# An unused 64-byte tile among the constants: the address that weights and moving operands have modulo 512 bytes

## The chip, the cores and the metric

The kernel runs on one core of one Trainium2 chip. The metric is the device time of one execution, in microseconds (us). Beside the timed runs there is one profiled execution, from which all traces and profile pages here come.

## The reference

One layer of a hybrid mixer on 1024 latent tokens and 256 context tokens of width 1024, all in float32:

```python
h, gate = modulate(x, c, norm_g, w_ada, b_ada)          # RMSNorm, adaLN scale and shift
z  = h @ w_in                                           # 1024 x 1024 -> 1024 x 8704
ya = neighbourhood_attention(q, k, v, kc, vc, rpb) * silu(z_a)   # 16 x 64 grid, 8 x 16 window, + 256 context keys
yb = b * dw_conv(c_ * v_, w_short) * silu(z_b)          # short depthwise convolution, width 3
yc = silu(layer_norm(dw_conv(a * sigmoid(g), w_conf))) * silu(z_c)   # depthwise convolution, width 31
m  = ga * (ya @ w_out_a) + gb * (yb @ w_out_b) + gc * (yc @ w_out_c) # sigmoid gates, 1024 wide
x  = x + gate * (m @ w_o)
```

## The kernel before

The kernel keeps float32 accuracy by cutting every matrix operand into two float32r parts, `hi` and `lo` (a rounded copy made by ScalarE, and the rest by a subtraction on VectorE or GpSimd). Each product is three matmuls: `hi*hi`, `hi*lo`, `lo*hi`. Each matmul has its own weight load. Most have 128 x 128 weights and a moving operand of 128 x 512:

```python
106    def mm3(ps, terms):
109            pe.matmul(ps, ah, bh, start=i == 0, stop=False)
110            pe.matmul(ps, ah, bl, start=False, stop=False)
111            pe.matmul(ps, al, bh, start=False, stop=i == n - 1)
...
841    def product(ps, w, blocks, first, last):
846            pe.matmul(ps, wh, bh, start=first and j == 0, ...)
847            pe.matmul(ps, wh, bl, start=False, ...)
848            pe.matmul(ps, wl, bh, start=False, ...)
```

The second operand of `pe.matmul` is the weights, the third the moving operand. In the profile's rows the moving operand stands first: `gc<-T,wh` has moving `T` and weights `wh`.

The work, in the order of time in the profiled execution:

- **0 to 115 us**: norms, adaLN and the first query, key and value projection (L417 to L419), whose weights are the tokens `ha`/`hb` and whose moving operand is the weight matrix `wh`/`wl`, 384 wide. Beside it the first GLU (`glu_steps`, L291), with weights `grow`, `ghi`, `glo` and moving `ha`/`hb`, 512 wide.
- **115 to 521 us**: attention for four pairs of heads, and woven into it by the scheduler the projections of the next pair (L109 to L111 with `ps`, 384 wide), the GLUs 1 to 3 (L109 to L111 with `gps`, `aps`, 512 wide) and, from 340 us, the first quarters of the later products (`quarter_part`, L677 to L679, 512 wide).
- **521 to 890 us**: `group` (L864) after `group`, each a 2 x 2 block product in a seven-product scheme, all matmuls 512 wide (`product`, L846 to L848). VectorE adds the sums out of PSUM (L852, L895, L899), GpSimd and VectorE make weight sums and `lo` parts (L760, L763), and between them VectorE does the width-31 convolution, 124 steps of 128 x 1024 (`conv_steps`, L820 and L822), which ends at 820 us. The very first two products of this part take weights that were made ahead of time (`ah`, `al`, L794); all later ones take `wh` and `wl` from `wsplit` (L835).
- **890 to 1030 us**: three merges of the branches (`merge`, L1152), 12 matmuls for each of 16 half rows, and beside them the LayerNorm's column sums (L1213, L1214, weights `onesr`).
- **1030 to 1117 us**: the last product with `w_o` (`fin_first`, `fin_rest`), again `product`, and the output.

**Where the tiles lie.** SBUF tiles come from pools that are stacked from two ends. On the left lies first the pool of constants `cst`, whose size is the sum of its tiles; behind it `hT` (`ha0` to `ha7`, `hb0` to `hb7`: the moving operands of most products), and behind that the pools of each stage (`a1`, `st`, `at`; later `tp`, `sp`, `bp`). On the right lie `edge`, `rp`, and the pools that hold the weights: `w` up to 521 us and `wq` after it.

```python
53    cst = ctx.enter_context(tc.tile_pool(name="cst", bufs=1))
54    hp_pool = ctx.enter_context(tc.tile_pool(name="hT", bufs=1, reuse_waits="tile"))
55    edge = ctx.enter_context(tc.tile_pool(name="edge", bufs=1, side="right"))
56    edge.tile([P, 32], F32, name="edge")
57    rp = ctx.enter_context(tc.tile_pool(name="rp", bufs=6, side="right"))
59    wp = wctx.enter_context(tc.tile_pool(name="w", bufs=9, side="right"))
801    wq = ctx.enter_context(tc.tile_pool(name="wq", bufs=1, side="right", reuse_waits="tile"))
```

Addresses in the built program, in bytes within a partition. Nearly all tiles behind `cst` are multiples of 512 bytes long, and one column block of weights (128 float32r) is 512 bytes, so that whole groups of tiles share one address modulo 512:

| tiles | first address before | modulo 512 | in the changed kernel | modulo 512 |
|---|---|---|---|---|
| `ha0` (and all of `hT`) | 3360 | 288 | 3424 | 352 |
| `grow` (pool `a1`) | 81184 | 288 | 81248 | 352 |
| `T1` (pool `tp`) | 68896 | 288 | 68960 | 352 |
| `ah`, `al` (pool `sp`) | 136480 | 288 | 136544 | 352 |
| `qd`, `ks`, `vs`, `phi`, `pt` (pool `at`) | 147232 (`qd`) | 288 | 147296 | 352 |
| `wh`, `wl` (pool `w`) | 184672 | 352 | 184672 | 352 |
| `wh`, `wl` (pool `wq`) | 171872, 188256 | 352 | 171872, 188256 | 352 |
| `ident` (pool `cst`) | 1376 | 352 | 1376 | 352 |

So before, weights from `w` and `wq` lie 64 bytes above their moving operands modulo 512 (the **64 class**: L677 to L679, nearly all of L846 to L848, L109 to L111 with `gps`, `aps` and `ops`). In the projections the weights are the tokens and lie 64 bytes below their moving `wh`, `wl` (the **-64 class**). Where both operands come from the left pools they lie at one address (the **0 class**: attention's L586 to L596 and L634, the first GLU, the two products with `ah` and `al`, the column sums).

Of the kernel before, what the change touches and what calls it, by code (L numbers as in the profile page):

```python
# [8 lines left out]
F32 = mybir.dt.float32  # L9
# [8 lines left out]
P = 128  # L18
D = 1024
KT = 8  # L20
# [27 lines left out]
def tile_hybrid(ctx: ExitStack, tc, x, xT, cx, cond, crow, ng, w_ada, b_ada, wqkv, wz,  # L48
# [4 lines left out]
    cst = ctx.enter_context(tc.tile_pool(name="cst", bufs=1))  # L53
# [18 lines left out]
    def const(src, shape, name):  # L72
        t = cst.tile(shape, F32, name=name)
        nc.sync.dma_start(t, src)
        return t
# [232 lines left out]
    with tc.tile_pool(name="st", bufs=1) as st, tc.tile_pool(name="ps_t", bufs=1, space=PSUM) as pst:  # L308
# [14 lines left out]
            return t.rearrange("p (a n) -> p a n", a=2)  # L323

        cond_t = const(cond, [P, KT, 2], "cond_t")
        act.activation(cond_t, cond_t, AF.Silu)

        def silu_rows(i):
# [1160 lines left out]
def build(ins):  # L1489
    import concourse.bacc as bacc  # L1490

    nc = bacc.Bacc("TRN2", target_bir_lowering=False, num_devices=1, dynamic_dma_scratch_size=1024)
    aps = {n: nc.dram_tensor(f"in_{n}", v.shape, F32, kind="ExternalInput").ap() for n, v in ins.items()}
    out = nc.dram_tensor("out_0", (KT, P, S), F32, kind="ExternalOutput").ap()
    with tile.TileContext(nc, schedule_with_timeline_sim=True) as tc:
        tile_hybrid(tc, **aps, out=out)
    return nc
# [11 lines left out]
```

## Time and profile before

| | |
|---|---|
| median of 3 runs | 1121.47 us (1115.14 to 1122.44) |
| profiled execution, its own time | 1118.38 us |
| span of its trace | 1116.6 us |
| TensorE (PE) busy | 1083.6 us, 97% of the span, 5270 matmuls |
| weight loads (PEld) | 908.2 us |
| VectorE (DVE), GpSimd (POOL), ScalarE (ACT) busy | 787.4, 656.8, 551.3 us |
| mean granted TensorE clock | 0.992 |

A matmul's duration in the trace runs to its modelled end and overlaps the next matmul. How fast PE works through a queue of matmuls is therefore read from the starts: the **pitch**, the time from one matmul's start to the next one's.

### The profile page before, as it was taken

Reading aid. Unit: us, or ns where it says so; the run is one execution under the profiler, and the core shown is the slowest. Engines: PE = TensorE matmul, PEld = TensorE weight load, DVE = VectorE, ACT = ScalarE, POOL = GpSimd, SP = SyncE. Lnnn points to the kernel's source line nnn. Section 1 sums busy time; section 2 is a strip of 40 time slices with the busy share of each in tenths; the row PEclk is TensorE's granted clock in tenths of the full one; section 3 lists DMA queues with packets and bytes.
Section 4 is the critical chain, followed back from the end, with each engine's and each line's share of the span. In section 5 each row is a group of like instructions: output and inputs, shape, how many; then the busy total and the mean of one; then the engine's idle time right before and its main releaser. Section 6 shows DMA issues by size and latency. Waiting matters only on the chain.

```text
span 1116.6 us, 15993 instructions
## 1 busy us (share of the span) xinstructions
PE 1083.6 (97%) x5270; PEld 908.2 (81%) x5270; DVE 787.4 (71%) x1255; ACT 551.3 (49%) x1172; POOL 656.8 (59%) x666
## 2 busy tenths in 40 slices
PE   6899999999999999999999989999999999999998
PEld 5688898998998778887888768778888888788886
DVE  6985476667666754426995998997953459878664
ACT  6865566576567576655432233133344434425630
POOL 3245956447536963334998857887777461623660
PEclk8999999999999999999999989999999999999999
DMA  9629423213303454449456436466445988461362
GB/s 352 214 74 293 129 68 126 92 49 99 120 28 98 163 198 133 135 159 367 144 165 181 153 104 200 154 203 189 160 161 165 322 323 302 132 238 65 97 219 100
DMA packets 92995, 186.26 MB, mean 167 GB/s; under 512 B 11792, under 2 KB 36752, under 8 KB 92816
## 3 DMA queue, kind: packets, MB, share of 16 engines
q1 hardware_dynamic: 88304, 183.13, 48.9%
q10 hardware_dynamic: 4608, 2.10, 0.6%
q8 instruction: 42, 0.69, 0.3%
q14 instruction: 41, 0.34, 0.1%
HBM read 136.96 MB, written 50.79 MB: 168 GB/s over the span
## 4 chain that ended last, share of the span: by engine, by line
PE 75%; DVE 8%; DMA 6%; POOL 5%; issue 3%; ACT 2%; SPq 1%; POOLq 0%; DVEq 0%; ACTq 0%
PE ops L110 4%; PE ops L109 4%; PE ops L111 4%; PE gd L846 3%; PE gd L848 3%; PE gd L847 3%; PE qps L678 3%; PE qps L679 3%; PE qps L677 3%; PE py L634 3%; DVE cv L822 3%; PE pp L614 3%; PE ps L109 2%; PE ps L110 2%; PE ps L111 2%
## 5 line engine op out<-in xcount | busy, mean ns | idle before, releaser
L822 DVE SCALAR_TENSOR_TENSOR cv<-upad,cf_t,cv 128x1024 f32<-128x1024 f32 x120 | 153.5, 1279 | 1.0
L759 ACT CAST wh<-s 128x512 fp32r<-128x512 f32 x111 | 66.6, 616 | 133.2 <-POOL s L763 80.8
L92 POOL TENSOR_TENSOR wl<-wr,wh 128x384 fp32r<-128x384 f32 (+1 forms) x87 | 85.8, 992 | 73.2 <-ACT wh L90 58.9
L760 POOL TENSOR_TENSOR wl<-s,wh 128x512 fp32r<-128x512 f32 x83 | 113.6, 1379 | 11.8 <-ACT wh L759 11.8
L617 DVE TENSOR_TENSOR plo<-pp,phi 128x256 fp32r<-128x256 f32 (+2 forms) x96 | 54.4, 575 | 41.7 <-ACT phi L616 40.8
L90 ACT CAST wh<-wr 128x384 fp32r<-128x384 f32 (+1 forms) x96 | 45.8, 483 | 40.7 <-PE qps L678 23.4
L679 PE MATMUL qps<-ha,wl 128*128 128x512 f32 x160 | 64.0, 400 | 0.0
L678 PE MATMUL qps<-ha,wh 128*128 128x512 f32 x160 | 63.8, 399 | 0.0
L677 PE MATMUL qps<-ha,wh 128*128 128x512 f32 x160 | 63.7, 399 | 0.0
L573 POOL TENSOR_TENSOR bias<-mk,img 64x96 f32<-64x96 bf16 (+1 forms) x96 | 45.2, 477 | 26.6 <-DVE mn L599 18.1
L616 ACT CAST phi<-pp 128x256 fp32r<-128x256 f32 (+2 forms) x96 | 46.4, 494 | 21.6 <-PE pp L614 21.2
L760 POOL TENSOR_TENSOR wl<-wro,wh 128x512 fp32r<-128x512 f32 x12 | 17.1, 1425 | 55.8 <-ACT wh L759 48.7
L599 DVE CUSTOM_DVE_ANT_0 pt<-sl,bias,mn 128x384 f32<-128x384 f32 (+1 forms) x64 | 37.2, 581 | 17.1 <-PE sl L596 14.8
L614 PE MATMUL pp<-ident,pt 128*128 128x128 f32 x304 | 47.2, 272 | 1.0 <-DVE pt L607 1.0
L846 PE MATMUL gd<-hb,wh 128*128 128x512 f32 x96 | 39.3, 409 | 7.1 <-DVE c L852 7.1
L614 PEld LDWEIGHTS pp<-ident,pt 128*128 128x128 f32 x304 | 37.8, 141 | 9.5 <-issue 1.4
L600 ACT ACTIVATE pt<-sc,mn 128x256 f32<-128x256 f32 x64 | 30.5, 477 | 29.8 <-DVE mn L599 27.8
L80 POOL TENSOR_SCALAR ssh<-ssh 128x4 f32<-128x4 f32 (+1 forms) x40 | 10.2, 255 | 59.3 <-DVE ssh L255 56.5
L81 POOL TENSOR_TENSOR ssh<-ssh,half_neg 128x4 f32<-128x4 f32 (+1 forms) x40 | 39.9, 998 | 3.0
L760 DVE TENSOR_TENSOR wl<-s,wh 128x512 fp32r<-128x512 f32 x28 | 36.0, 1287 | 7.6 <-ACT wh L759 7.5
L607 DVE TENSOR_SCALAR pt<-pt,mn 128x640 f32<-128x640 f32 (+1 forms) x64 | 40.5, 675 | 1.0
L109 PE MATMUL ps<-wh,hb 128*128 128x384 f32 x112 | 38.9, 348 | 0.5 <-ACT raw L175 0.4
(439 smaller groups left out, 3793.7 us busy)
## 6 DMA issues: line engine op xcount, KB each, us to landing
wr<-in_wz SPq DMA_DIRECT2D x34, 512.0 KB, 3.9
gs<-gd SPq DMA_DIRECT2D x24, 512.0 KB, 5.2
wr<-in_wz SPq DMA_DIRECT2D x52, 192.0 KB, 2.5
wada<-in_w_ada SPq DMA_DIRECT2D x16, 512.0 KB, 8.6
wrf<-in_wo SPq DMA_DIRECT2D x16, 512.0 KB, 3.5
cht<-chd SPq DMA_DIRECT2D x24, 256.0 KB, 3.1
wro<-in_wout SPq DMA_DIRECT2D x24, 256.0 KB, 4.3
p1d<-quarter SPq DMA_DIRECT2D x20, 256.0 KB, 2.5
```

Source lines behind the costliest of these rows:

```text
L92: lo_eng.tensor_tensor(out=lo[:, :n], in0=raw[:, :n], in1=hi[:, :n].bitcast(F32), op=ALU.subtract)
L109: pe.matmul(ps, ah, bh, start=i == 0, stop=False)
L110: pe.matmul(ps, ah, bl, start=False, stop=False)
L111: pe.matmul(ps, al, bh, start=False, stop=i == n - 1)
L614: pe.transpose(out=pp[:, c * P : c * P + P], in_=src, identity=ident)
L677: pe.matmul(ps, wh, bh, start=k == 0, stop=False, skip_group_check=True)
L678: pe.matmul(ps, wh, bl, start=False, stop=False, skip_group_check=True)
L679: pe.matmul(ps, wl, bh, start=False, stop=k % 4 == 3, skip_group_check=True)
L759: act.copy(hi, src)
L760: eng.tensor_tensor(out=lo, in0=src, in1=hi.bitcast(F32), op=ALU.subtract)
L822: dve.scalar_tensor_tensor(out=acc, in0=src, scalar=cf_t[:, i, j : j + 1], in1=acc, op0=ALU.mult, op1=ALU.add)
L846: pe.matmul(ps, wh, bh, start=first and j == 0, stop=False, skip_group_check=True)
```

## The change

A tile of 128 x 8 x 2 float32, 64 bytes in each partition, is taken from `cst` behind `cond_t`. Nothing writes or reads it. The constants allocated behind it, and every pool of the left side, move up by 64 bytes; the right side and the constants ahead of it stay. All instructions, their order on every engine and their waits are the same in both programs; only addresses differ. In the changed kernel the 64 class and the -64 class both become the 0 class.

```diff
         cond_t = const(cond, [P, KT, 2], "cond_t")
+        cst.tile([P, KT, 2], F32, name="sig")
         act.activation(cond_t, cond_t, AF.Silu)
```

## The prediction

> **What bounds the kernel now.** I read the page first: the span, the busy time and the chain that ended last.
>
> ```profile
> span 1116.6 us, 15993 instructions
> PE 1083.6 (97%) x5270; PEld 908.2 (81%) x5270; DVE 787.4 (71%) x1255; ACT 551.3 (49%) x1172; POOL 656.8 (59%) x666
> PE 75%; DVE 8%; DMA 6%; POOL 5%; issue 3%; ACT 2%; SPq 1%; POOLq 0%; DVEq 0%; ACTq 0%
> ```
>
> TensorE carries three quarters of the chain, so what a matmul costs in a full queue decides. Its duration doesn't say that; the pitch does. The timeline of PE around 521 us, where the 64 class and the 0 class follow each other, is the most telling view of this trace (columns: start us, duration us):
>
> ```profile
> 519.53 0.39 PE L679 MATMUL qps<-ha,wl 128*128 128x512 f32 x1
> ...
> 521.63 0.40 PE L679 MATMUL qps<-ha,wl 128*128 128x512 f32 x1
> 521.86 0.39 PE L846 MATMUL ga<-ha,ah 128*128 128x512 f32 x1
> ...
> 522.55 0.39 PE L846 MATMUL ga<-ha,ah 128*128 128x512 f32 x1
> ...
> 527.31 0.40 PE L846 MATMUL gc<-T,wh 128*128 128x512 f32 x1
> ...
> 540.62 0.39 PE L846 MATMUL gf<-T,wh 128*128 128x512 f32 x1
> ```
>
> From 519.53 to 521.63 stand 9 matmuls of the 64 class: 2.10 us, a pitch of 233.3 ns. From 522.55 to 527.31 stand 21 matmuls with `ah` and `al`, the 0 class: 4.76 us, **226.7 ns**. From 527.31 to 540.62 it is the 64 class again, 57 matmuls in 13.31 us: **233.5 ns**. Same lines of code, same width, moving operands from the same tiles. The first three of the 0 class (521.86 to 522.55) took 230 ns each; the fast pitch needs a run of them. Two more stretches, the first GLU (0 class) and the last merge (64 class), say the same:
>
> ```profile
> 57.47 0.39 PE L109 MATMUL gps<-ha,grow 128*128 128x512 f32 x1
> ...
> 60.87 0.39 PE L109 MATMUL gps<-ha,grow 128*128 128x512 f32 x1
> ```
>
> ```profile
> 1000.20 0.39 PE L110 MATMUL ops<-ycl,wh 128*128 128x512 f32 x1
> ...
> 1029.83 0.40 PE L111 MATMUL ops<-ych,wl 128*128 128x512 f32 x1
> ```
>
> 57.47 to 60.87 is 15 matmuls of the 0 class, 226.7 ns; 1000.20 to 1029.83 is 127 of the 64 class, 233.3 ns, nearly five hundred microseconds after the first and under other neighbours. So I take **6.6 ns** as the difference of the two classes for a 512-wide matmul in a run, and 3.3 ns (233.3 less 230) for the first three of one. The weight load that could meet with the stream starts together with it:
>
> ```profile
> 519.53 0.19 PEld L677 LDWEIGHTS qps<-ha,wh 128*128 128x128 f32 x1
> ```
>
> This load, for the next matmul, starts at 519.53 like the matmul L679 above: two reads of SBUF side by side, whose distance modulo 512 is what the change sets. That this meeting is the cause is my inference; the pitches are measured.
>
> **The change, part by part.** It adds no instruction and no wait and moves none on any queue; it takes 64 bytes and turns the 64 class into the 0 class. Its worth is a count of matmuls times 6.6 ns, as far as PE sets the pace. By stage:
>
> ```profile
> 370.00:521.60 151.60, 149.34 (x738) 122.31 (x737) 73.10 (x145) 94.99 (x229) 75.03 (x83) 1.00 0.55 187
> 527.30:600.00 72.70, 72.70 (x313) 58.58 (x312) 67.22 (x68) 23.90 (x40) 65.66 (x50) 1.00 0.55 178
> 600.00:743.00 143.00, 135.94 (x569) 108.20 (x568) 128.70 (x123) 42.50 (x72) 109.03 (x86) 0.98 0.48 157
> 743.00:890.00 147.00, 147.00 (x631) 118.44 (x631) 96.63 (x114) 61.18 (x108) 103.38 (x80) 1.00 0.60 198
> 890.00:1117.00 227.00, 222.83 (x952) 178.57 (x951) 164.13 (x264) 89.14 (x157) 96.88 (x73) 1.00 0.54 186
> ```
>
> (Columns: stretch, its length, then busy us and count of PE, weight loads, VectorE, ScalarE, GpSimd; granted clock, share of DMA, GB/s.)
>
> *Late, 743 us to the end.* PE is busy without a gap up to the output's tail. The two rows count 631 and 952 matmuls; less 36 of the LayerNorm (32 column sums, which are 0 class already, and 4 others) that leaves 1547. No other engine is at its limit (VectorE 97 of 147 us, then 164 of 227). 1547 x 6.6 ns = **10.2 us**, nearly all of it on the path.
>
> *Middle, 527 to 743 us.* 313 and 569 matmuls, 882 x 6.6 ns = 5.8 us of PE time. But here PE waits, and the chain of this stretch isn't PE's:
>
> ```profile
> PE gd L846 <- DVE c L852: 7.1, 4, 3.6
> ```
>
> ```profile
> by line: DVE cv L822 20.9%; issue 17.9%; DVE wl L760 9.5%; POOL wl L760 5.9%; POOL s L763 5.6%; DVE c L852 5.0%; PE gd L846 4.4%; PE gd L848 3.9%; PE gd L847 3.9%; DVE by L1088 3.3%; POOL zb L1094 3.1%; DMA ysd<-zb 2.9%; DVE v L899 2.4%; DM
> ```
>
> The first row (wait, us in total, times, longest) is of 520 to 760 us: four times the `gd` product waits for VectorE's sum L852, which stands behind convolution steps. VectorE alternates between full and idle stretches:
>
> ```profile
> 560.00:580.00 20.00, 20.00 (x87) 16.14 (x86) 19.93 (x20) 5.67 (x9) 18.64 (x13) 1.00 0.49 155
> 600.00:620.00 20.00, 20.00 (x88) 16.10 (x87) 12.88 (x14) 6.87 (x11) 15.45 (x12) 1.00 0.52 160
> 660.00:680.00 20.00, 20.00 (x87) 16.14 (x86) 19.89 (x21) 6.55 (x11) 15.75 (x12) 1.00 0.34 114
> 680.00:700.00 20.00, 20.00 (x87) 16.10 (x87) 15.74 (x18) 7.90 (x14) 11.70 (x13) 1.00 0.72 235
> 720.00:740.00 20.00, 20.00 (x87) 16.04 (x86) 19.96 (x19) 5.78 (x10) 18.69 (x14) 1.00 0.48 162
> ```
>
> Where VectorE is full (19.9 of 20), a faster PE only comes to L852 earlier and waits longer; where it has room (12.9 and 15.7 of 20), PE's progress releases it, and the gain stays. About a third of this stretch is of the second kind: I take **2 us** of 5.8, and 0 and 5.8 as the bounds. What is late next here is the convolution, L822.
>
> *Early, 120 to 521 us.*
>
> ```profile
> L679 PE MATMUL qps<-ha,wl 128*128 128x512 f32 x160 | 64.0, 400 | 0.0
> L109 PE MATMUL gps<-ha,wh 128*128 128x512 f32 x24 | 9.8, 409 | 0.0
> ```
>
> ```profile
> by line: PE qps L678 21.4%; PE qps L677 21.4%; PE qps L679 21.3%; DMA hb<-td 7.4%; PE py L634 6.8%; PE pp L614 6.2%; DVE pt L607 2.8%; PE sl L595 1.8%; DVE hb L742 1.5%; PE sl L596 1.5%; issue 1.3%; ACT hb L741 1.3%; PE sc L586 1.1%; PE sc
> ```
>
> 160 on each of the lines L677 to L679, and 24 for each of the twelve such rows of GLUs 1 to 3 (three lines, two tensors, two halves): 768 matmuls, at most 5.1 us. They stand between attention's transposes and narrow matmuls, which break the runs (3.3 instead of 6.6 ns for the first three), and of 370 to 520 us, where most are, the row above (shares of the chain) gives their lines 64%. I take half, **2.5 us**; bounds 0 and 5.1.
>
> *What I cost at nothing.* The projections go from the -64 to the 0 class:
>
> ```profile
> 211.24 0.34 PE L111 MATMUL ps<-wh,ha 128*128 128x384 f32 x1
> ...
> 212.45 0.34 PE L109 MATMUL ps<-wh,ha 128*128 128x384 f32 x1
> ```
>
> ```profile
> L109 PE MATMUL ps<-wh,hb 128*128 128x384 f32 x112 | 38.9, 348 | 0.5 <-ACT raw L175 0.4
> L109 PE MATMUL ps<-wh,ha 128*128 128x384 f32 x96 | 32.5, 340 | 0.0
> L596 PE MATMUL sl<-ks,qlz 128*128 128x384 f32 x48 | 16.2, 337 | 0.0
> ```
>
> Seven of them took 1.21 us, 173 ns each, and attention's 384-wide matmuls of the 0 class last 337 ns against 340 and 348: no class stands out, 3 ns either way. On 624 of them (112 and 96 on three lines) that is 1.9 us up or down, the bound I also take for the transposes, whose `ident` gets its data's address. GpSimd's `lo` parts read one tile of the left and one of the right pools, which now share an address too:
>
> ```profile
> L760 POOL TENSOR_TENSOR wl<-s,wh 128x512 fp32r<-128x512 f32 x83 | 113.6, 1379 | 11.8 <-ACT wh L759 11.8
> L760 POOL TENSOR_TENSOR wl<-wro,wh 128x512 fp32r<-128x512 f32 x12 | 17.1, 1425 | 55.8 <-ACT wh L759 48.7 <-DMA gd<-pz 7.1
> L760 POOL TENSOR_TENSOR wl<-wrf,wh 128x512 fp32r<-128x512 f32 x8 | 10.4, 1300 | 17.9 <-ACT wh L759 17.9
> ```
>
> `s` lies 64 bytes off `wh` and takes 1379 ns; `wro` and `wrf` lie at its address and take 1425 and 1300. The class doesn't order them, so nothing is charged; it is hidden anyway beside PE after 743 us, and 50 ns more on 83 would be 4 us of GpSimd, felt only before that.
>
> *Sum.* 10.2 + 2 + 2.5 = 14.7 us. The profiled execution took 1118.4 us (span 1116.6 and 1.8 around it), so **1103.7 us**; the median of the runs shown is 3.1 above that execution and the lowest 3.2 below, so I say **1104** for the new median. All 3197 matmuls at 6.6 ns would be 21.1 us.
>
> **The rivals.**
>
> *The address doesn't matter.* Every slow run has its weights in the right pools and every fast one in the left, so the trace can't part distance modulo 512 from the place itself. If the place decides, nothing changes: **1118 to 1122**. For it: this confusion. Against it: the bare distance doesn't order them, since `ah` lies 133 KB above `ha0` and is fast, while `wh` lies 103 KB above `T1` and is slow (addresses in the table); and the fast weights are of two pools, `grow` 55 KB below `ah`. Chance 0.12. [...]
>
> *VectorE takes it all up to 820 us.* The convolution runs until then; after a faster 743 to 820 us (77 / 0.2333 = 330 matmuls, 2.2 us) PE could meet it again, and the middle and early gains be swallowed. Left are 890 to 1117 us and a little: 952 x 6.6 = 6.3, up to 9 us: **1109 to 1113**. For it: VectorE's full stretches. Against: 97 of 147 us after 743. Chance 0.08. A further price hangs on it:
>
> ```profile
> 647.79 0.63 PE L847 MATMUL gd<-hb,wh 128*128 128x512 f32 x1
> ...
> 652.49 0.63 PE L846 MATMUL gd<-T,wh 128*128 128x512 f32 x1
> ```
>
> After its longest wait, 3.6 us, PE ran 11 matmuls at 427 ns, the time of the clock's drop (0.98 in the row of 600 to 743 us); 194 ns x 11 is 2.1 us. If a longer wait brought a second drop, as much again would go. [...]
>
> *Equal addresses collide, slower.* It could be the common 288 of the left pools that is good, not their equality, and two reads that start together at one address of the right pools' 352 could meet at every step. Priced by the one step that the classes show, 6.6 ns more instead of less on 3197 matmuls: 21 us, **1139**. It decides if the pitch after 743 us is above 233.3 ns. Against: `ah` and `grow` are equal to their streams and fast. Chance 0.05.
>
> **How the numbers follow.** The forecast has 0.75, with its own range of 1096 to 1112: 21.1 us and the 1.9 us of the projections give 1095.4 at best; the late part alone, with 3 us of the runs' spread, gives 1111. The range for 8 in 10 adds the second rival and what lies between: **1095 to 1116**. One per cent is 11 us, about what a measurement of this kernel can tell from no change. Of the forecast's cases some 0.64 gain more than that (the late part and 1 us more), with a little of the second rival **0.66 faster**; the rest of both and the first rival make **0.29 the same**; the third makes **0.05 slower**.
>
> **What would show it.** Right: pitches of 226 to 227 ns in long runs after 743 us (233.3 before), 1547 of them, the last matmul 10 us earlier counted from there; the `gd` waits for L852 grow from 7.1 us; projections stay at 173 ns. Wrong: a pitch of 233 that stays (first rival), fast pitches with PE waits after 743 us (second), or above 233 (third).

## The result, and the profile after

The changed kernel takes **1104.18 us** (median of 6 runs, 1102.29 to 1105.11); the kernel before took 1120.74 us (6 runs, 1115.14 to 1125.03). The ratio is 0.9851, with a 95% interval of 0.9824 to 0.9879: 1.2 to 1.8% faster. The profiled execution took 1104.47 us, 13.9 us less than that of before. The top of its page (span; busy time of each engine; chain that ended last):

```profile
span 1102.4 us, 15993 instructions
PE 1069.0 (97%) x5270; PEld 912.0 (83%) x5270; DVE 777.3 (71%) x1255; ACT 549.9 (50%) x1172; POOL 653.8 (59%) x666
PE 71%; DMA 9%; DVE 6%; POOL 6%; issue 4%; ACT 3%; SPq 1%; POOLq 0%; ACTq 0%; DVEq 0%
```

The same instructions, and PE is busy 14.6 us less. Lines behind the added one have numbers one higher: L846 is now L847, L852 is L853. The timeline of PE in the changed kernel (start, duration), first at the place where the prediction read 57 matmuls of the 64 class, then in the last merge:

```profile
526.69 0.39 PE L847 MATMUL gc<-T,wh 128*128 128x512 f32 x1
...
539.61 0.39 PE L847 MATMUL gf<-T,wh 128*128 128x512 f32 x1
...
990.14 0.39 PE L111 MATMUL ops<-ych,wl 128*128 128x512 f32 x1
...
1019.83 0.39 PE L110 MATMUL ops<-ycl,wh 128*128 128x512 f32 x1
```

57 matmuls in 12.92 us are 226.7 ns each (233.5 before), and 131 in 29.69 us are 226.6 ns (233.3 before). The former 64 class now has the pitch that `ah`, `al` and `grow` had all along.

To see where the time was won, I take the same matmul in both timelines at the end of each stage. Before (its matmul at 521.63 stands in the prediction):

```profile
115.03 0.34 PE L111 MATMUL ps<-wh,ha 128*128 128x384 f32 x1
...
743.06 0.40 PE L846 MATMUL gd<-hb,wh 128*128 128x512 f32 x1
...
890.06 0.40 PE L846 MATMUL ge<-hb,wh 128*128 128x512 f32 x1
...
1112.43 0.40 PE L848 MATMUL fd<-mb,wl 128*128 128x512 f32 x1
```

After:

```profile
117.66 0.33 PE L111 MATMUL ps<-wh,ha 128*128 128x384 f32 x1
...
521.02 0.39 PE L680 MATMUL qps<-ha,wl 128*128 128x512 f32 x1
...
737.84 0.39 PE L847 MATMUL gd<-hb,wh 128*128 128x512 f32 x1
...
880.64 0.39 PE L847 MATMUL ge<-hb,wh 128*128 128x512 f32 x1
...
1098.26 0.39 PE L849 MATMUL fd<-mb,wl 128*128 128x512 f32 x1
```

The changed kernel was profiled a second time in the last experiment. The same matmuls there:

```profile
117.97 0.33 PE L111 MATMUL ps<-wh,ha 128*128 128x384 f32 x1
...
521.18 0.39 PE L680 MATMUL qps<-ha,wl 128*128 128x512 f32 x1
...
737.26 0.39 PE L847 MATMUL gd<-hb,wh 128*128 128x512 f32 x1
...
880.06 0.39 PE L847 MATMUL ge<-hb,wh 128*128 128x512 f32 x1
...
1096.26 0.39 PE L849 MATMUL fd<-mb,wl 128*128 128x512 f32 x1
```

| stage | before, us | after, us | gain, us | gain in the second profile, us | forecast, us |
|---|---|---|---|---|---|
| start to 115 | 115.03 | 117.66 | -2.6 | -2.9 | 0 |
| early, to 521 | 406.60 | 403.36 | 3.2 | 3.4 | 2.5 |
| middle, to 743 | 221.43 | 216.82 | 4.6 | 5.35 | 2 |
| late, to the last matmul | 369.37 | 360.42 | 8.95 | 10.4 | 10.2 |
| sum | 1112.43 | 1098.26 | 14.2 | 16.2 | 14.7 |

The late row splits at 890 us: 147.00 less 142.80 is 4.2 us there, which is 631 matmuls of 6.6 ns, all of it kept; 222.37 less 217.62 is 4.75 us behind it, where some 916 matmuls promised 6.0. In the second profile the same two stretches gain 4.2 and 6.2 us.

PE's waits of the changed kernel from 500 to 1120 us (us in total, times, longest):

```profile
PE gd L847 <- DVE c L853: 8.2, 4, 3.4
PE sums L1215 <- DVE lnl L761: 0.9, 2, 0.6
```

The first was 7.1 us before: in this execution VectorE's sums took back only 1.1 us of the middle stage. The second is new. PE reaches the LayerNorm's column sums before VectorE has made their `lo` parts (waits of 0.26 us ahead of 909.16 and 0.61 us ahead of 917.30 in the timeline). Counted as gaps in the pitch that costs about 1.3 us: the part of the late gain that is missing in this execution.

Neither row holds for every profile. The second profile of the change has 6.9 us for VectorE's sums and no wait at the column sums; the kernel with both sides moved (second experiment), whose pitch is the slow one, waits longest at the column sums. Their rows of the same stretch:

```profile
PE gd L847 <- DVE c L853: 6.9, 4, 3.3
```

```profile
PE sums L1215 <- DVE lnl L761: 2.0, 1, 2.0
```

### The profile page after: what moved, and what is told of

Read it like the earlier page. It is cut to its first block, busy times and chain, and to the rows that moved or that the text cites. A ratio compares the mean times of both kernels' runs of the same rounds, so it can differ in the third digit from the quotient of the medians.

```text
span 1102.4 us, 15993 instructions
## 1 busy us (share of the span) xinstructions
PE 1069.0 (97%) x5270; PEld 912.0 (83%) x5270; DVE 777.3 (71%) x1255; ACT 549.9 (50%) x1172; POOL 653.8 (59%) x666
## 4 chain that ended last, share of the span: by engine, by line
PE 71%; DMA 9%; DVE 6%; POOL 6%; issue 4%; ACT 3%; SPq 1%; POOLq 0%; ACTq 0%; DVEq 0%
PE ops L111 4%; PE ops L109 4%; PE ops L110 4%; PE qps L679 3%; PE qps L680 3%; PE qps L678 3%; PE gd L847 3%; PE gd L848 3%; PE gd L849 3%; PE py L635 3%; PE ps L109 3%; PE ps L110 3%; PE ps L111 3%; PE pp L615 2%; DMA wada<-in_w_ada 2%
## 5 line engine op out<-in xcount | busy, mean ns | idle before, releaser
L761 POOL TENSOR_TENSOR wl<-wro,wh 128x512 fp32r<-128x512 f32 x12 | 16.8, 1398 | 54.5 <-ACT wh L760 47.9
L847 PE MATMUL gd<-hb,wh 128*128 128x512 f32 x96 | 38.7, 403 | 8.2 <-DVE c L853 8.2
L109 PE MATMUL ps<-wh,hb 128*128 128x384 f32 x112 | 38.8, 347 | 0.6 <-ACT rawc L224 0.5
L849 PE MATMUL gd<-hb,wl 128*128 128x512 f32 x96 | 38.4, 400 | 0.0
```

The costliest lines, as they stand in the source:

```text
L761: eng.tensor_tensor(out=lo, in0=src, in1=hi.bitcast(F32), op=ALU.subtract)
L847: pe.matmul(ps, wh, bh, start=first and j == 0, stop=False, skip_group_check=True)
L849: pe.matmul(ps, wl, bh, start=False, stop=last and j == 3, skip_group_check=True)
```

## The experiments

**The distance, made from the other side.** Nothing is added on the left; the right pools move instead.

```diff
-    edge.tile([P, 32], F32, name="edge")
+    edge.tile([P, 48], F32, name="edge")
         cond_t = const(cond, [P, KT, 2], "cond_t")
-        cst.tile([P, KT, 2], F32, name="sig")
```

> The kernel before with 64 bytes added at the right end (tile `edge` 48 instead of 32 floats) and no unused tile among the constants: the left pools stay at 288 modulo 512, the weights move down to 288, so that weights and streams again lie at one address. Distance theory: the same gain as the change, 1104 us (1101 to 1107), pitch of long 512-wide runs after 743 us 226.7 ns. Rival, it is the left pools' place at 352 that is good: no gain, 1117 to 1124 us, pitch 233.3 ns.

Measured: 1102.0 us (4 runs, 1099.78 to 1103.76), the kernel before 1118.92 (14 runs); ratio 0.9862, 0.9838 to 0.9887. The last merge in PE's timeline:

```profile
988.23 0.39 PE L110 MATMUL ops<-ycl,wh 128*128 128x512 f32 x1
...
1017.92 0.39 PE L109 MATMUL ops<-ych,wh 128*128 128x512 f32 x1
```

131 matmuls, 226.6 ns. Both operands lie at 288 here and both at 352 in the changed kernel, with one result. It is the distance.

**Both sides moved.** The unused tile stays, and the weights move up by the same 64 bytes.

```diff
-    edge.tile([P, 32], F32, name="edge")
+    edge.tile([P, 16], F32, name="edge")
```

> The changed kernel, unused tile kept, with 64 bytes taken from the right end (tile `edge` 16 instead of 32 floats): the left pools stay at 352, the weights move up to 416, again 64 above their streams. Distance theory: the gain is undone, 1120 us (1116 to 1125), pitch 233.3 ns. Rival, the left pools' place or anything else about the unused tile: 1104 us, pitch 226.7 ns.

Measured: 1118.48 us (10 runs, 1115.98 to 1121.43), ratio 1.0003, 0.9984 to 1.0023. The last merge:

```profile
1000.12 0.39 PE L109 MATMUL ops<-ych,wh 128*128 128x512 f32 x1
...
1029.98 0.39 PE L111 MATMUL ops<-ych,wl 128*128 128x512 f32 x1
```

128 matmuls, 233.3 ns. Moving the left pools by 64 bytes gives nothing when the weights follow. The first rival (the place decides, or nothing does) falls.

**64 bytes below instead of above.**

```diff
-        cst.tile([P, KT, 2], F32, name="sig")
+        cst.tile([P, KT, 4], F32, name="sig")
```

> The changed kernel with an unused tile of 128 instead of 64 bytes: left pools at 416, weights at 352, now 64 bytes below their streams in the products and 64 above in the projections. Distance theory, if only the size of the distance counts: 1120 us, pitch 233.3 ns. [...] Place theory (left pools away from 288 are good): 1104 us.

Measured: 1107.52 us (5 runs, 1106.7 to 1111.89), ratio 0.9920, 0.9891 to 0.9949. The last merge:

```profile
990.22 0.39 PE L111 MATMUL ops<-ych,wl 128*128 128x512 f32 x1
...
1019.97 0.39 PE L109 MATMUL ops<-ych,wh 128*128 128x512 f32 x1
```

130 matmuls, 228.8 ns. The sign counts: weights 64 bytes below their stream cost 2 ns, 64 above cost 6.6. That fits the projections, whose weights lay 64 below before and showed no class of their own: at their width of 384 the map below has the same pitch, 173.35 ns, at 64 below as at 0.

**The pitch by distance, measured by itself.** A small kernel of matmul blocks, 30 in each, at chosen distances; one execution.

> Not the layer: 37 blocks of 30 matmuls each, float32r unless said, that sweep the distance of weights above moving operand from 0 to 480 bytes in steps of 32, at 4, 8, 16 and 48, for weights or streams or both in the right half of SBUF (0 and 64 bytes), for widths 384, 256 and 128 (0, 64 and 448 bytes), for weights that alternate between 0 and 64, and for bfloat16 (0, 64, 128 bytes). Distance theory: pitch at 512 wide 226.7 ns at 0 and 233.3 at 64, wherever weights and streams lie; alternating something between; other distances unknown, 216 to 240 ns. Place theory: the blocks with weights in the right half are slow at 0 too.

PE's timeline groups each block (start, duration, count); the next block's start less this one's, by 30, is the mean pitch. In the names `near` has both operands in one pool, the letters a, b, c ... are distances of 0, 32, 64 ... bytes (so i is 256, j is 288), `half` is bfloat16 at 0, 64 and 128 bytes:

```profile
16.61 6.97 PE L38 MATMUL neara<-m,w 128*128 128x512 f32 x30
23.42 7.15 PE L38 MATMUL nearb<-m,w 128*128 128x512 f32 x30
30.41 7.16 PE L38 MATMUL nearc<-m,w 128*128 128x512 f32 x30
37.41 7.18 PE L38 MATMUL neard<-m,w 128*128 128x512 f32 x30
...
72.28 7.00 PE L38 MATMUL neari<-m,w 128*128 128x512 f32 x30
79.12 7.15 PE L38 MATMUL nearj<-m,w 128*128 128x512 f32 x30
...
247.25 6.64 PE L38 MATMUL halfb<-bm,bw 128*128 128x512 bf16 x30
253.72 6.64 PE L38 MATMUL halfc<-bm,bw 128*128 128x512 bf16 x30
```

At 0 the block takes 6.81 us (227.0 ns), at 32 6.99 and at 64 7.00 (233.3); at 256 it is 6.84, near the fast one again; bfloat16 at 64 takes 6.47 (215.7). The last 20 matmuls of each block, single in the timeline, leave the first slower ones out:

| weights above stream, bytes | 0 | 32 | 64 | 96 | 128 | 160 | 192 | 224 | 256 |
|---|---|---|---|---|---|---|---|---|---|
| pitch at 512 wide, ns | 226.65 | 233.35 | 233.35 | 234.3 | 232.45 | 233.45 | 228.75 | 233.3 | 226.7 |

From 256 on the row repeats (480 bytes: 233.35). So the period of this map is **256 bytes**, and 0 is the one fully fast distance among those tried; 4, 8, 16 and 48 bytes gave 232.65, 230.7, 233.25 and 233.3. Weights far off, streams far off, or both, gave 226.7 at 0 and 233.3 at 64: the place made no difference. 384 wide it is 173.35 at 0, 176.7 at 64 and 173.35 at 448 (64 below); 256 wide 120.0, 117.8, 117.75, so there the order turns round; 128 wide 111.65 at all three. bfloat16 took 215.85 ns at 0, 64 and 128: no distance showed in it. Weights that alternate between 0 and 64 took 232.45 ns, nearly the slow pitch, where I had expected something between.

**256 bytes off, in the layer.**

```diff
-        cst.tile([P, KT, 2], F32, name="sig")
+        cst.tile([P, KT, 10], F32, name="sig")
```

> The changed kernel with an unused tile of 320 instead of 64 bytes: left pools at 96 modulo 512, weights at 352, so 256 bytes apart. If the distance counts modulo 512: no better than before, 1119 us, 233 ns. If, as the map of pitches has it (226.7 ns at 0 and at 256), it counts modulo 256: the whole gain, ratio 0.985 to 0.987, 226.7 ns after 743 us.

Measured: 1104.26 us (4 runs, 1103.73 to 1104.47), the kernel before 1118.87 (7 runs); ratio 0.9868, 0.9840 to 0.9897. The last merge:

```profile
990.28 0.39 PE L109 MATMUL ops<-ych,wh 128*128 128x512 f32 x1
...
1019.98 0.39 PE L111 MATMUL ops<-ych,wl 128*128 128x512 f32 x1
```

131 matmuls, 226.7 ns: as fast as with one address modulo 512. The change's "modulo 512" asks for more than is needed.

**32 bytes off, in the layer.** One execution first, then ten more.

```diff
-        cst.tile([P, KT, 2], F32, name="sig")
+        cst.tile([P, KT, 1], F32, name="sig")
```

> The changed kernel with an unused tile of 32 instead of 64 bytes: left pools at 320, weights at 352, 32 bytes above their streams. By the map (233.35 ns at 32): half way brings nothing, 1116 to 1122 us, 233.3 ns after 743 us. If nearness counted in proportion: 1112 us, 230 ns.

> The same kernel as the one look at 32 bytes, timed. That look had the slow pitch (233.0 ns after 743 us) but 1111.84 us, since PE had no drop of its clock between 640 and 720 us. Distance theory: over several runs the ratio to before is 1.00 (0.995 to 1.003), and single runs spread by some 7 us as those of before do. If 32 bytes really bring something in time without a faster pitch: ratio 0.990 to 0.994.

The first execution took 1111.84 us, below what I expected, though the pitch after 743 us was slow. The ten: 1113.34 us (10 runs, 1111.76 to 1117.15), the kernel before 1118.26 (13 runs, 1112.37 to 1124.16); ratio 0.9971, 0.9949 to 0.9993. Its last merge, its PE waits and a window of its middle stage:

```profile
995.29 0.40 PE L111 MATMUL ops<-ych,wl 128*128 128x512 f32 x1
...
1024.92 0.40 PE L109 MATMUL ops<-ych,wh 128*128 128x512 f32 x1
```

```profile
PE gd L847 <- DVE c L853: 3.3, 3, 1.8
```

```profile
600.00:680.00 80.00, 79.72 (x342) 63.94 (x341) 71.52 (x73) 26.54 (x45) 62.02 (x52) 1.00 0.47 154
```

127 matmuls at 233.3 ns: no gain by pitch, as the map says of 32. The 0.3% comes from elsewhere. In the profiled execution PE waited 3.3 us for VectorE in place of 7.1, and the clock (third figure from the end) stayed at 1.00. The whole lead of that execution, 6.5 us at the last matmul, arises between 626 and 660 us, where the kernel before has its wait of 3.6 us and then its clock drop. Why VectorE was less late there stays open; the kernel before spreads over 12 us in its own 13 runs.

**Which reads meet.** A second small kernel, one execution. In `ownzero` each matmul's weights lie at distance 0 from its own stream and 64 off from its neighbours'; in `nextzero` at 0 from the neighbouring streams and 64 off from their own. `run` blocks follow an interruption by narrow matmuls; `t` blocks try 64 placements of the `lo` parts in the order of `product`.

> Not the layer: blocks of matmuls in float32r, 512 wide. In `ownzero` each matmul's weights lie at its own stream's address modulo 512, and the next weights 64 off the running stream; in `nextzero` the next weights lie at the running stream's address and its own 64 off. If the load of the next weights beside the running stream is what collides: `ownzero` 233, `nextzero` 226.7 ns. If the own weights' distance counts: the reverse. `run` blocks of 12 behind 3 matmuls of 256: the first three to six near 230 ns, then 226.7. The `t` blocks have the order hi*hi, hi*lo, lo*hi of the products, with the lo weights (second letter) and the lo streams (third letter) moved by 0 to 224 bytes in steps of 32: if some pair lets the three loads miss each other better than at 0, a pitch below 226.7 ns; else 226.7 at aa alone and up to 235 elsewhere.

PE's timeline, grouped by block:

```profile
17.60 7.11 PE L30 MATMUL ownzero<-m,w 128*128 128x512 f32 x30
24.55 7.12 PE L30 MATMUL nextzero<-m,w 128*128 128x512 f32 x30
31.50 0.52 PE L30 MATMUL gapa<-m,w 128*128 128x256 f32 x3
```

Both took 6.95 us, 231.7 ns. Neither the weights' own stream nor the neighbour's alone brings the fast pitch; the test did not separate my two explanations, and it speaks against each in its simple form. Five of the six `run` blocks gave 234, 235, 229, 232 and 231 ns before 227 and 226, and the first needed nine matmuls to come down to 226: behind such an interruption these runs took five to nine matmuls to become fast. Of the 64 placements only all parts at distance 0 reached 226.65 ns; the next best had 227.95, the worst 233.95. The changed kernel's placement is the best of those.

**The waits that were left.** The changed kernel with two convolution steps in place of three behind each group's last sum, and the changed kernel again beside it:

```diff
         use1(0, add(d, u2, "c21"))
-        conv_step(3)
+        conv_step(2)
```

> The changed kernel with two instead of three convolution steps at the end of each group (line 917 of before), against PE's waits for VectorE's sum (8.2 us in four waits, and a drop of the clock of 2.6 us behind the longest). If those waits come from convolution steps ahead of the sum: waits under 4 us, no drop, 1094 to 1100 us. If they come from elsewhere (GpSimd's splits, loads), or the steps left over to the end of the stage cost as much: 1101 to 1108 us.

> The changed kernel once more, on this chip beside the other two: ratio to before 0.982 to 0.988, 1100 to 1107 us. It is what the kernel with fewer convolution steps has to beat.

Measured: 1100.77 us (4 runs, 1100.3 to 1102.85), ratio 0.9851, 0.9815 to 0.9886; the change again 1102.25 (4 runs, 1100.54 to 1102.47), ratio 0.9862, 0.9832 to 0.9892. PE's waits with fewer steps:

```profile
PE gd L847 <- DVE c L853: 6.1, 6, 2.1
PE gd L847 <- DVE pz L853: 1.2, 2, 0.9
PE sums L1215 <- DVE lnl L761: 0.4, 1, 0.4
```

I had expected under 4 us of waits and 1094 to 1100 us. The long wait went (2.1 instead of 3.4 and 3.3), but six short ones and two of another kind stand in place of four: 7.3 us in all, against 8.2 and 6.9 in the two profiles of the change. I had also expected no drop of the clock; it came behind the wait of 2.1 us, seven matmuls from 628.16 at 426 ns. The two versions can't be told apart.

## Why the prediction held, point by point

*What bounds the kernel.* PE's pitch, not the matmul's duration, was the right reading: the number 226.7, read from 21 matmuls of before, is what 131 of the last merge now take. That distance and not place makes the classes was an inference in the prediction; the two moves of the right pools and the small kernel show it.

*Late: 10.2 us forecast, 8.95 and 10.4 measured.* Count and price held to 890 us (4.2 of 4.2 us). This stretch, in which PE waits for nothing, is the cleanest test of the price. Between the same two matmuls the gain over before is 4.2 us in all four profiles with weights at 0 or 256 bytes (the change twice, right pools moved, 256 off), 2.8 us at 64 below, and 0.0 in the three with weights 64 or 32 bytes above (both sides moved, 32 off twice). Behind 890 us the first profile lacks 1.3 us at the column sums, which VectorE releases; I had counted these sums out of the gain without asking what releases them. The second profile has no such wait. That a faster PE causes it is not shown, since the longest one, 2.0 us, stands in the kernel with both sides moved.

*Middle: 2 us forecast, 4.6 and 5.35 measured*, inside the bounds of 0 and 5.8. This is the term that I mis-sized. I had taken stretches in which VectorE is full as stretches that give nothing back, and I had read a row of the chain that is of 600 to 741 us alone as that of the whole stage. From 520 to 600 us the chain of before is PE's:

```profile
by line: PE gd L846 10.5%; PE gd L848 10.5%; PE gd L847 10.5%; PE gc L846 7.0%; PE gc L847 7.0%; PE gf L846 7.0%; PE gf L848 7.0%; PE gf L847 7.0%; PE gc L848 6.7%; PE ge L846 5.8%; PE ge L848 5.8%; PE ge L847 5.8%; PE ga L847 2.3%; PE ga L
```

PE has 313 matmuls from 527 to 600 us without any wait, although VectorE is full there in part. Two matmuls that were 72.80 us apart before (527.31 and 600.11) are 70.72 us apart in both profiles of the change: 2.1 us, already all that I charged for the stage. Behind 600 us stand four waits. In the first profile they grew by 1.1 us, and 5.8 less 1.1 is 4.7; in the second they did not grow. How much a faster PE lengthens them is not shown: the four profiles with the fast pitch have 6.6 to 8.2 us of these waits, the four with the slow pitch 3.3 to 7.1. Waits, with the clock drops behind them, move this stage as much as the whole term: the three slow-pitch profiles other than before's pass it 1.8, 5.3 and 6.6 us faster than that one did. (The experiments ran on three chips; how much of this scatter is the chip's is not known.)

*Early: 2.5 forecast, 3.2 and 3.4 measured*, inside 0 and 5.1, but the agreement of the stage is partly luck. The three slow-pitch profiles gain 1.8 to 2.5 us in the same stage. Most of that comes from 120 to 137 us: there before's execution has three waits of PE, 1.6 us together, and every other profile of the layer has one of 0.5 to 0.6. The pitch can be read by itself, between starts less than 260 ns apart: `qps` went from 233.0 to 229.2 ns (379 pairs), the GLUs 1 to 3 from 232.9 to 229.7 (226 pairs), together 2.2 us. So half of the 6.6 ns was a good price here.

*The cost of nothing.* Between starts less than 200 ns apart, the projections' 384-wide matmuls (L109 to L111) took 174.4 ns in the mean against 173.6 before, which on 624 of them is 0.5 us, inside the 1.9 us allowed. The small kernel gives 173.35 ns both at 0 and at 64 below, so no change was the right charge. GpSimd's `lo` parts, whose operands now share an address, took 1379 ns before; in the costliest groups after:

```profile
L761 POOL TENSOR_TENSOR wl<-s,wh 128x512 fp32r<-128x512 f32 x83 | 113.5, 1378 | 7.6 <-ACT wh L760 7.6
```

*What was not in the sum: the start.* The first 115 us took 2.6 us longer. The windows of that stretch, before, after, and with both sides moved:

```profile
0.00:115.00 115.00, 97.47 (x523) 84.63 (x524) 85.91 (x173) 75.62 (x149) 48.46 (x72) 0.96 0.66 231
```

```profile
0.00:115.00 115.00, 98.59 (x509) 85.87 (x509) 84.12 (x170) 73.43 (x144) 45.19 (x71) 0.93 0.65 229
```

```profile
0.00:115.00 115.00, 98.21 (x509) 85.74 (x509) 84.93 (x170) 72.92 (x144) 44.84 (x70) 0.93 0.64 228
```

The granted clock was 0.93 against 0.96. The kernel with both sides moved has it too, with its 64 class untouched, so equal addresses are not its condition. Among the profiles here 0.93 and 0.96 both recur, each kernel that was profiled twice with the same one; the cause stays open. The clock is not the whole of it either. Of the 2.6 us, 1.6 are lost by 46 us (granted clock from 30 to 45 us 0.89 against 1.00), and 1.0 at 115 us, where PE waits 0.9 us for VectorE's `ks`; the kernel 32 bytes off, timed, loses 1.7 us at that place with a clock of 0.96. Without the loss at the start the sum would have been 16.8 us. That the total of the first profile came out within half a microsecond is thus partly luck, errors that cancel: -2.6, +0.7, +2.6 and -1.3. The second profile gained 16.2 us, and the medians of the runs differ by 16.6. The new median still met the forecast of 1104 because the prediction set out from an execution of 1118.4 us, 2.4 below the median that the kernel before had beside it.

*The rivals.* "VectorE takes it all" is wrong: 743 to 890 us kept its whole gain. The second clock drop that it named did not come in the profiled execution of the changed kernel; the one drop moved:

```profile
707.81 0.63 PE L848 MATMUL gd<-hb,wh 128*128 128x512 f32 x1
...
712.07 0.63 PE L849 MATMUL gd<-hb,wl 128*128 128x512 f32 x1
```

426 ns for each of these, behind the wait of 3.4 us. In the second profile there are two drops, seven matmuls from 628.64 and six from 707.38; together they are about as long as the one of before, so the further 2.1 us of that rival did not come. "Equal addresses collide" is wrong at the right pools' 352 (after) and at 288 (right pools moved). That the address doesn't matter is wrong for 512-wide float32r matmuls: the small kernel shows 226.65 and 233.35 ns with nothing but the distance changed. For bfloat16 it shows 215.85 at each distance tried.

## What to carry to other kernels

Where PE works through a full queue, compare the pitch of like matmuls from start to start in every stage: two values at one width are a price list, and the count of matmuls times the difference is the gain, as long as nothing else ends the stage. For the 512-wide float32r matmuls here, weights and moving operands at one address modulo 256 bytes were the fast case (226.65 ns at 0, 226.7 at 256, 228.75 to 234.3 at the steps of 32 bytes between), and that for both `hi` and `lo` (226.65 ns with all parts at 0, 227.95 at best with the `lo` parts elsewhere). A pool's start depends on every tile ahead of it, so here 64 unused bytes gave 1.5% (ratio 0.9851). In the middle stage VectorE took back only what PE's waits for it grew by (1.1 us in the first profile, nothing in the second), and the stretch from 527 to 600 us, where it is full in part, still gave 2.1 us; but ask also what releases the instructions that the faster engine reaches next. Read the price where the engine doesn't wait: the middle stage, with its waits, differed by up to 6.6 us between profiles of the slow pitch, and one pair of profiles can't size it.

## What was not expected of the hardware

- In the map the pitch repeats after 256 bytes (226.65 ns at 0, 226.7 at 256), the sign counts (192 bytes, which is 64 below: 228.75 ns; 64 above: 233.35), and at 256 wide the distance of 0 is the slower one (120.0 against 117.8 ns).
- In the second small kernel the fast pitch came only five to nine matmuls behind an interruption (234, 235, 229, 232 and 231 ns before 227), and distance 0 to the weights' own stream alone, or to the neighbour's alone, left it at 231.7 ns. That two reads meet was an inference; no run shows which, or that they do.
- The clock drop does not follow from the length of the last wait alone. In the second profile of the change PE ran seven matmuls at 426 ns each behind a wait of 2.52 us; in the first, behind a wait of 2.48 us at the same place, the next matmuls have the fast pitch (226.5 ns for 17 of them from 629.51):

```profile
628.20 0.64 PE L847 MATMUL gd<-hb,wh 128*128 128x512 f32 x1 [2.52 <-DVE c L853]
```

```profile
628.74 0.47 PE L847 MATMUL gd<-hb,wh 128*128 128x512 f32 x1 [2.48 <-DVE c L853]
```

In the kernel with fewer convolution steps a drop came just behind a wait of 2.10 us too (seven matmuls at 426 ns), and the one drop of before came behind its wait of 3.6 us (11 matmuls at 427 ns). With a drop behind 2.10 and 2.52 us and none behind 2.48, the length of one wait is not the whole condition; what the rest of it is, no run shows.
